# Stick-breaking heads scored in pairs, their recurrence sums taken from two rounded parts

## The chip, the cores and the metric

One core of a Trainium2 chip runs the whole program. The metric is the device time of one execution in microseconds (us); the median of the runs shown is what the change is judged by.

## What is computed

Two layers on 256 tokens of width 1024. Each is a mixer, a layer norm, a mixture of 16 experts (two chosen for each token) and another layer norm. The change lies in the mixer of layer 0, whose left half is a stick-breaking attention with 8 heads of width 64 over two blocks of 128 queries:

```python
z = jnp.einsum('bqhd,bkhd->bhqk', q[:, q0:kend], k[:, :kend]).astype(jnp.float32) * scale
mask = s[None, :] < t[:, None]
log_1mb = jnp.where(mask, -jax.nn.softplus(z), 0.0)
after = lax.cumsum(log_1mb, axis=3, reverse=True) - log_1mb
w = jnp.where(mask, jnp.exp(jax.nn.log_sigmoid(z) + after), 0.0)
outs.append(jnp.einsum('bhqk,bkhd->bqhd', w.astype(v.dtype), v[:, :kend]))
```

Its right half is a state-space recurrence (S5): 32 groups of 16 channels with 64 complex states, `x_l = a x_(l-1) + B u_l`, `y_l = Re(C x_l) + D u_l`, then gelu and a gate. Both halves meet in one output projection.

## The kernel before

Everything is transposed: channels on the partitions, the 256 tokens in the free dimension. Weights come in tiles of 1 MB (`u`, 20 of them) on SyncE's one DMA queue, in the order of use. Plain f32 matmuls run beside matmuls on fp32r operands: where a product must keep f32's precision at fp32r's cost, the operands are split into a rounded part and a rest (`split`, L195) and multiplied in three steps (`mm3`, L203 to L205).

Layer 0's mixer (`mixer0`) runs in this order on TensorE. First the projections to `u`, `v`, then `k` and `q` in four pieces of 128 rows, two heads in each (L986). Then the attention and the recurrence, woven into each other, up to L958, where the recurrence's output is made. Then the output projection (L203 to L205), the gate and the rest of the projection.

The attention comes from `stick`, which returns three functions.
- `scores(h)`, called `S(h)`: one head's logits in a bank of PSUM (`z`, from the pool `acc` of 4 banks). Two matmuls on 64 rows, the upper half of the partitions or the lower, and two bf16 matmuls that add the mask (L1223). ScalarE takes Abs, Exp and Ln of it (L1226, L1228, L1229), VectorE makes the softplus `sp` (L1230), a tile of 128x384 f32 in the pool `b2` of 12 tiles.
- `weights(h)`, `W(h)`: three f32 matmuls with the constant matrices `ntri` sum `sp` over the keys on top of `z` (L1235), ScalarE takes Exp (L1240).
- `values(hp)`, `O(hp)`: four matmuls for two heads, one head to each half of a bank's partitions (L1251), from the pool `mm` of 4 banks.

The recurrence goes by `s5_transpose` (32 transposes on TensorE, L896, in eight banks of `mm` that ScalarE empties, L897), `s5_inputs` (64 matmuls of 32 columns into two banks, L906), `s5_states` and `s5_output` (L958). `s5_states` is a generator on VectorE with six steps, each drawn by one `n(states)`: the first two turn the inputs (L921 to L923), the next two are scans (L930, L932), the fifth and the sixth write the real and the imaginary half of the states `X` (L921 to L923 again, on 128x496). `X` lies in the upper half of the tile `vx`, which held the rows of `u` and then the block matrix of the kernel before.

A scheduler sets each engine's order from the order in which the calls are written, the dependences and the pools; every engine then works through its own list in order, and a wait at its head holds what stands behind. `follow` adds an order between two instructions: `self.cut` holds a split's second part (L195) behind the instruction that it names.

## Time and profile before

| | us |
|---|---|
| median of 3 runs (763.88 to 766.96) | 764.04 |
| the profiled execution | 768.54 |
| its span, first instruction to last | 766.9 |
| TensorE busy in the span | 743.6 |
| VectorE, ScalarE, GpSimd busy | 327.9, 207.2, 46.6 |

How to read it: the page gives each engine's busy time, the span in 40 slices, and the groups of instructions with the mean duration of one. A matmul's duration includes its way through the array, so matmuls overlap, and what one costs in a row of them is the distance from its start to the next one's. An f32 matmul stands in the trace as two records. The timeline merges neighbours of one kind into a row: start, length, number, and in brackets the idle time before it. PE is TensorE, DVE is VectorE, ACT is ScalarE, POOL is GpSimd, SP is SyncE.

### The profile page before, as it was taken

What the parts mean: (1) busy time and instruction counts of PE and PEld (TensorE: products, weight loads), DVE (VectorE), ACT (ScalarE), POOL (GpSimd) and SP (SyncE); (2) the same over time, 40 slices, a digit from 0 to 9 for tenths busy, and PEclk for the clock granted to TensorE, in tenths of its full rate; (3) what the DMA queues carried; (4) which work ended last, traced back from release to release, by engine and by line L of the source; (5) the groups of instructions that cost most, each with busy time, mean ns of one, the idle gap of its engine ahead of it and who ended that gap; (6) DMA issues with size and microseconds to landing.
All of it is one profiled execution on the core that took longest, in us unless ns stands there. A gap on an engine that the chain in (4) does not pass through costs nothing. (4 is left out here: it accounts for less than half of the span.)

```text
span 766.9 us, 10505 instructions
## 1 busy us (share of the span) xinstructions
PE 743.6 (97%) x4115; PEld 419.7 (55%) x4115; DVE 327.9 (43%) x836; ACT 207.2 (27%) x421; POOL 46.6 (6%) x45
## 2 busy tenths in 40 slices
PE   8999999999999999999999999999999999999993
PEld 6588778643534335343878665677535335344332
DVE  9992647711222112124947798835312112221123
ACT  1344435212102001002625575733111001011002
POOL 1010000001000000000020142200002000000000
PEclk9999999999999999999999998999999999999998
DMA  8839879889999999999985100298799999999941
GB/s 322 303 111 195 310 272 409 308 279 378 396 424 421 420 421 421 421 417 421 420 309 194 56 1 0 70 399 306 245 361 417 383 421 421 423 420 420 421 171 59
DMA packets 42539, 241.00 MB, mean 314 GB/s; under 512 B 8144, under 2 KB 9680, under 8 KB 15568
## 3 DMA queue, kind: packets, MB, share of 16 engines
q1 hardware_dynamic: 42480, 240.23, 80.1%
q8 instruction: 34, 0.56, 0.3%
q14 instruction: 25, 0.20, 0.1%
HBM read 238.38 MB, written 1.84 MB: 313 GB/s over the span
## 5 line engine op out<-in xcount | busy, mean ns | idle before, releaser
L493 PE MATMUL mm<-u,s 128*64 128x512 f32 x960 | 214.3, 595 | 0.0
L493 PEld LDWEIGHTS mm<-u,s 128*64 128x64 f32 x960 | 66.6, 137 | 129.6 <-issue 121.7
L523 PE MATMUL mm<-u,b 128*64 128x512 f32 x512 | 113.1, 593 | 0.0
L528 ACT ACTIVATE b<-mm,gslot 128x512 fp32r<-128x512 f32 x32 | 22.0, 687 | 259.3 <-PE mm L523 259.3
L529 DVE SCALAR_TENSOR_TENSOR b<-mm,gslot,b 128x512 fp32r<-128x512 f32 x32 | 24.0, 751 | 146.5 <-ACT b L528 146.5
L523 PEld LDWEIGHTS mm<-u,b 128*64 128x64 f32 x512 | 36.3, 137 | 72.0 <-issue 70.2
L195 DVE TENSOR_TENSOR s<-u,s 128x1024 fp32r<-128x1024 f32 x37 | 45.9, 1248 | 29.4 <-ACT s L192 29.3
L572 DVE TENSOR_TENSOR b<-b,mm 128x256 f32<-128x256 f32 x32 | 12.0, 417 | 91.7 <-PE mm L493 72.7
L192 ACT ACTIVATE s<-u 128x1024 fp32r<-128x1024 f32 x37 | 38.7, 1056 | 43.6 <-PE acc L205 30.6
L986 PE MATMUL mm<-u,u 128*128 128x256 f32 x208 | 46.5, 381 | 1.9 <-DMA u<-w_in 1.9
L986 PEld LDWEIGHTS mm<-u,u 128*128 128x128 f32 x208 | 39.0, 190 | 9.0 <-issue 1.9
L354 ACT ACTIVATE s<-mm,c_k_all 128x256 f32<-128x256 f32 x32 | 18.1, 564 | 81.6 <-PE mm L469 81.6
L203 PE MATMUL acc<-s,u 128*128 128x512 f32 x96 | 38.7, 403 | 0.5 <-ACT u L1206 0.5
L469 PE MATMUL mm<-b,u 128*128 128x256 f32 x160 | 39.1, 326 | 0.0
L205 PE MATMUL acc<-s,u 128*128 128x512 f32 x96 | 38.3, 399 | 0.0
L204 PE MATMUL acc<-s,u 128*128 128x512 f32 x96 | 38.3, 398 | 0.0
L534 PE MATMUL acc<-b,b 128*128 128x512 f32 x128 | 33.5, 399 | 0.0
L469 PEld LDWEIGHTS mm<-b,u 128*128 128x128 f32 x160 | 29.9, 190 | 6.6 <-issue 4.9
L592 DVE COPY b<-mm 128x512 f32<-128x512 f32 x16 | 11.1, 692 | 46.3 <-PE mm L591 46.2
L534 PEld LDWEIGHTS acc<-b,b 128*128 128x128 f32 x128 | 22.6, 189 | 7.8 <-issue 3.2
L356 DVE TENSOR_SCALAR s<-mm,c_k_all 128x256 f32<-128x256 f32 x32 | 16.8, 542 | 22.9 <-PE mm L469 22.7
L469 PE MATMUL mm<-b,s 128*128 128x256 f32 x96 | 23.5, 285 | 0.0
(309 smaller groups left out, 1010.5 us busy)
## 6 DMA issues: line engine op xcount, KB each, us to landing
u<-moe SPq DMA_DIRECT2D x180, 1024.0 KB, 12.5
u<-w_in SPq DMA_DIRECT2D x26, 1024.0 KB, 16.1
u<-w_in SPq DMA_DIRECT2D x10, 512.0 KB, 6.7
s<-moe SPq DMA_DIRECT2D x4, 1024.0 KB, 5.7
b<-moe SPq DMA_DIRECT2D x16, 256.0 KB, 8.2
u<-moe SPq DMA_DIRECT2D x8, 512.0 KB, 16.8
u<-xT SPq DMA_DIRECT2D x4, 256.0 KB, 5.5
out<-u SPq DMA_DIRECT2D x4, 256.0 KB, 4.4
```

The source lines that it names most:

```text
L192: a = self.nc.scalar.activation(s[:, 0], x, AF.Copy)
L195: self.mark = self.nc.vector.tensor_tensor(s[:, 1], x, s[:, 0].bitcast(F32), ALU.subtract)
L203: mm(o, l[0], r[0], start=first, stop=False, skip_group_check=True)
L204: mm(o, l[0], r[1], start=False, stop=False, skip_group_check=True)
L205: self.tail = mm(o, l[1], r[0], start=False, stop=last, skip_group_check=True)
L469: nc.tensor.matmul(pg[:, 0:T], x[:, t, k * P:(k + 1) * P], g.bitcast(F32) if m == 1 else g, start=(i == 0), stop=(i == 2 * m - 1))
L493: self.mark = nc.tensor.matmul(h[c * 64:(c + 1) * 64], xe[:, k, e + c], w[c], start=(k == 0), stop=(k == KC - 1))
L523: self.mark = nc.tensor.matmul(y[c * 64:(c + 1) * 64], hx[:, f, c * 64:(c + 1) * 64], w[:, c * 512:c * 512 + 512], start=(f == 0), stop=(f ...
L528: nc.scalar.activation(yh, y, AF.Copy, scale=gs)
L529: nc.vector.scalar_tensor_tensor(yl, y, gs, yh.bitcast(F32), ALU.mult, ALU.subtract)
L534: self.tail = nc.tensor.matmul(out[half][t], sT[:, t * P:(t + 1) * P], yy, start=False, stop=(p == 7 and j == 1), skip_group_check=True)
L986: self.mark = self.nc.tensor.matmul(ps, w[:, k * P:k * P + P], xT[:, k], start=(k == 0), stop=(k == KC - 1))
```

## The change

`scores` takes a pair of heads, `hp`. Both heads' first parts (256 columns) are issued one behind the other, one on the upper 64 rows and one on the lower, then both second parts (128 columns), then the four mask matmuls. VectorE rounds each head's `sp` to fp32r (`hi`) and takes the rest (`lo`), two tiles of `b2` more for each head; the pool has 15 tiles for 12. `weights` multiplies each of the three column ranges by `hi` and by `lo`, six fp32r matmuls for three f32 ones, against `tr`, an fp32r copy of `ntri` that ScalarE makes once. The weights' Exp is written over `sp`. The calls stand in another order: the first half of the pairs before the third piece of `k` and `q`, all scores before the recurrence's inputs, and `self.cut` is set to the last `lo` of the first two pairs. Five `n(states)` stand where there were six, so that the sixth step, which writes the imaginary half of `X`, is not issued; the readers of that half find what the tile held.

```diff
@@ -33,7 +33,7 @@
 NOSYNC = mybir.DependencyInfo(mybir.DependencyClass.NoSync, mybir.DependencyReason.DATA)
 NU = 20
 NS = 3
-N2 = 12
+N2 = 15
 WARM = 3
 ORD = {mybir.EngineType.PE}
 WARM0 = 5
@@ -1150,21 +1150,21 @@
         self.s5_toeplitz(self.s5_kernel(ca, vx[:, 1].rearrange("p (a r n) -> p a r n", a=16, r=2)), kts)
         S(0), S(1)
         kq(2)
-        S(2), S(3)
-        kq(3)
-        W(0), S(4)
+        cols(k_out(3))
+        W(0), W(1)
+        cols(q_out(3))
+        S(2), W(2), W(3)
         self.s5_transpose(bbp[0], w1t[0])
-        W(1), S(5)
+        S(3)
         self.s5_transpose(bbp[1], w1t[1])
-        O(0), W(2)
+        O(0)
         self.stage(10)
         ps = self.s5_inputs(U, w1t)
         self.issue(CAP[1])
         states = self.s5_states(ps, X, bbp[1].rearrange("p a d h -> p (a d h)").rearrange("p (j n) -> p j n", j=4))
         ys = self.s5_output(U, X, kts, ca, w1t[0].rearrange("p a n -> p (a n)"))
         n = lambda g: next(g, None)
-        n(states), W(3), O(1), S(6), n(states), W(4), n(states), S(7), n(states), W(5), O(2), n(states), W(6), n(states)
-        W(7), O(3)
+        n(states), W(4), W(5), O(1), n(states), W(6), W(7), n(states), O(2), n(states), O(3), n(states)
         self.table("sigmoid_and_others")
         n(ys), n(ys)
         yT = n(ys)
@@ -1212,31 +1212,46 @@
 
         nc = self.nc
         st = {}
-
-        def scores(h):
-            s = slice((h % 2) * 64, (h % 2) * 64 + 64)
-            z = self.acc()
-            k, q = kT[s, h // 2], qT[s, h // 2]
-            nc.tensor.matmul(z[:, 0:T], k[:, 0:P], q, start=True, stop=False, skip_group_check=True)
-            nc.tensor.matmul(z[:, T:T + P], k[:, P:T], q[:, P:T], start=False, stop=False, skip_group_check=True)
-            for c in (0, T):
-                nc.tensor.matmul(z[:, c:c + P], self.identb, self.negb, start=False, stop=False, skip_group_check=True)
-
-            sp = self.b2((P, 384))
-            a = nc.scalar.activation(sp, z[:, 0:384], AF.Abs)
-            self.follow(a, self.logs)
-            nc.scalar.activation(sp, sp, AF.Exp, scale=-1.0)
-            nc.scalar.activation(sp, sp, AF.Ln, bias=1.0)
-            nc.vector.scalar_tensor_tensor(sp, z[:, 0:384], 0.0, sp, ALU.max, ALU.add)
-            st[h] = (z, sp)
+        tr = self.b2((P, 2, P), F32R)
+        nc.scalar.activation(tr, self.ntri, AF.Copy)
+
+        def scores(hp):
+
+            zs = [self.acc() for _ in range(2)]
+            rows = [slice(c * 64, c * 64 + 64) for c in range(2)]
+            for part in range(2):
+                for z, s in zip(zs, rows):
+                    k, q = kT[s, hp], qT[s, hp]
+                    if part == 0:
+                        nc.tensor.matmul(z[:, 0:T], k[:, 0:P], q, start=True, stop=False, skip_group_check=True)
+                    else:
+                        nc.tensor.matmul(z[:, T:T + P], k[:, P:T], q[:, P:T], start=False, stop=False, skip_group_check=True)
+            for z in zs:
+                for c in (0, T):
+                    nc.tensor.matmul(z[:, c:c + P], self.identb, self.negb, start=False, stop=False, skip_group_check=True)
+            for c, z in enumerate(zs):
+
+                sp = self.b2((P, 384))
+                hi, lo = [self.b2((P, 384), F32R) for _ in range(2)]
+                a = nc.scalar.activation(sp, z[:, 0:384], AF.Abs)
+                self.follow(a, self.logs)
+                nc.scalar.activation(sp, sp, AF.Exp, scale=-1.0)
+                nc.scalar.activation(sp, sp, AF.Ln, bias=1.0)
+                nc.vector.scalar_tensor_tensor(sp, z[:, 0:384], 0.0, sp, ALU.max, ALU.add)
+                nc.vector.tensor_copy(hi, sp)
+                low = nc.vector.tensor_tensor(lo, sp, hi.bitcast(F32), ALU.subtract)
+                if hp < 2:
+                    self.cut = low
+                hl = (hi, lo, sp)
+                st[hp * 2 + c] = (z, hl)
 
         def weights(h):
-            z, sp = st[h]
-            mm = lambda o, l, r, stop: nc.tensor.matmul(z[:, o[0]:o[1]], l, r, start=False, stop=stop, skip_group_check=True)
-            mm((0, T), self.ntri[:, 0], sp[:, 0:T], False)
-            mm((P, T), self.ntri[:, 1], sp[:, T:T + P], True)
-            mm((T, T + P), self.ntri[:, 0], sp[:, T:T + P], True)
-            w = self.b2((P, 384))
+            z, hl = st[h]
+            for o, l, c, n in ((0, 0, 0, T), (P, 1, T, P), (T, 0, T, P)):
+                for j in range(2):
+                    nc.tensor.matmul(z[:, o:o + n], tr[:, l], hl[j][:, c:c + n], start=False, stop=o > 0 and j == 1,
+                                     skip_group_check=True)
+            w = hl[2]
             nc.scalar.activation(w, z[:, 0:384], AF.Exp)
             st[h] = w
```

What the scheduler makes of it, at three places. TensorE, behind the recurrence kernel's matmuls (L869): before, head by head (`acc_478` and `acc_488` are the logits of heads 0 and 1, `u_255` holds `k` and `q`, `c_k_bits` the mask):

```order
L1220 MATMUL acc_478<-u_255 128x256
L1221 MATMUL acc_478<-u_255 128x128
L1223 LDWEIGHTS c_k_bits
L1223 MATMUL acc_478<-c_k_bits 128x128
L1223 LDWEIGHTS c_k_bits
L1223 MATMUL acc_478<-c_k_bits 128x128
L1220 MATMUL acc_488<-u_255 128x256
L1221 MATMUL acc_488<-u_255 128x128
```

TensorE at the same place after it (`acc_480` and `acc_481` are heads 0 and 1):

```order
L1226 MATMUL acc_480<-u_255 128x256
L1226 MATMUL acc_481<-u_255 128x256
L1228 MATMUL acc_480<-u_255 128x128
L1228 MATMUL acc_481<-u_255 128x128
L1231 LDWEIGHTS c_k_bits
L1231 MATMUL acc_480<-c_k_bits 128x128
L1231 LDWEIGHTS c_k_bits
L1231 MATMUL acc_480<-c_k_bits 128x128
```

The two heads' matmuls on 64 rows now stand side by side, and the mask matmuls on all rows follow for both. The second pair stands right behind.

TensorE behind the recurrence's inputs (L906), before: the sums of head 3 (L1235), and between the four value matmuls of heads 2 and 3 (L1251, `mm_744`) the scores of head 6 (`acc_751`):

```order
L1235 MATMUL acc_531<-b_54_536,b_14_237 128x256
L1235 MATMUL acc_531<-b_54_536,b_14_237 128x128 x2
L1251 MATMUL mm_744<-b_73_652,u_249 64x256
L1220 MATMUL acc_751<-u_255 128x256
L1251 MATMUL mm_744<-b_83_742,u_249 64x256
L1251 MATMUL mm_744<-b_73_652,u_249 64x128
L1251 MATMUL mm_744<-b_83_742,u_249 64x128
L1221 MATMUL acc_751<-u_255 128x128
```

TensorE at the values of heads 2 and 3 after it (`mm_820`; `hi` is `b_73_616`, `lo` is `b_74_617` of head 5, `b_82_673` and `b_83_674` are those of head 6, `b_36_375` is `tr`):

```order
L1252 MATMUL acc_597<-b_73_616,b_36_375 128x128
L1252 MATMUL acc_597<-b_74_617,b_36_375 128x128
L1266 MATMUL mm_820<-b_55_518,u_249 64x256
L1266 MATMUL mm_820<-b_58_527,u_249 64x256
L1266 MATMUL mm_820<-b_55_518,u_249 64x128
L1266 MATMUL mm_820<-b_58_527,u_249 64x128
L1252 MATMUL acc_662<-b_82_673,b_36_375 128x256
L1252 MATMUL acc_662<-b_83_674,b_36_375 128x256
```

No score stands behind L906 any more, and the value matmuls of all four pairs stand together. Before, those of three pairs were parted, once by a score and twice by a matmul of L259.

VectorE at the recurrence's end, before: the scans, two heads' softplus (L1230), and the fifth and the sixth step (`u_249` holds `X`), then the rests of the values (L1253):

```order
L930 SCALAR_TENSOR_TENSOR u_251<-b_12_234,u_251 128x512
L1230 SCALAR_TENSOR_TENSOR b_86_756<-acc_751,b_86_756 128x384
L932 SCALAR_TENSOR_TENSOR u_251<-b_12_234,u_251 128x512
L1230 SCALAR_TENSOR_TENSOR b_89_776<-acc_771,b_89_776 128x384
L921 TENSOR_TENSOR u_251<-u_251,u_84 128x16x31
L922 TENSOR_TENSOR u_251<-u_251,u_84 128x16x31
L923 TENSOR_TENSOR u_249<-u_251 128x16x31
L921 TENSOR_TENSOR u_251<-u_251,u_84 128x16x31
L922 TENSOR_TENSOR u_251<-u_251,u_84 128x16x31
L923 TENSOR_TENSOR u_249<-u_251 128x16x31
L1253 TENSOR_TENSOR u_256<-mm_642,u_256 128x256
```

VectorE from the scans on after it:

```order
L930 SCALAR_TENSOR_TENSOR u_251<-b_12_234,u_251 128x512
L932 SCALAR_TENSOR_TENSOR u_251<-b_12_234,u_251 128x512
L921 TENSOR_TENSOR u_251<-u_251,u_84 128x16x31
L922 TENSOR_TENSOR u_251<-u_251,u_84 128x16x31
L923 TENSOR_TENSOR u_249<-u_251 128x16x31
L1268 TENSOR_TENSOR u_256<-mm_714,u_256 128x256
```

The two softplus are gone from here (all eight stand ahead of the scans, one rounding and one rest of head 7 between the first steps of the recurrence), and of the two times three products of the last two steps three are left. Behind L958 the lists of TensorE, VectorE, ScalarE and GpSimd read alike before and after, to the end of the program. On SyncE's queue one half-tile of the projection's weights moves from ahead of the 16 small transfers of the recurrence kernel to behind them.

## Rows read from the trace of the kernel before

**Rows 1.** The page: TensorE's busy share in 40 slices.
```profile
PE   8999999999999999999999999999999999999993
```
**Rows 2.** TensorE's waits from 50 to 151 us: total, times, longest.
```profile
PE mm L345 <- DVE u L304: 0.8, 1, 0.8
...
PE acc L1220 <- ACT b L1240: 0.2, 1, 0.2
```
**Rows 3.** Busy time by stretch: engines, granted clock, DMA share, GB/s.
```profile
83.50:99.20 15.70, 15.70 (x103) 11.73 (x99) 12.53 (x20) 7.57 (x16) 0.00 (x0) 1.00 0.80 276
...
220.00:340.00 120.00, 120.00 (x592) 50.21 (x590) 21.89 (x49) 13.12 (x22) 0.00 (x0) 1.00 1.01 421
```
**Rows 4.** Timeline of TensorE: sums of head 0, scores of head 4.
```profile
69.94 1.04 PE L1235 MATMUL acc<-b,b 128*128 128x256 f32 x6
70.81 0.71 PE L896 MATMUL mm<-c_k_all,u 128*128 128x128 f32 x5
71.56 0.70 PE L1220 MATMUL acc<-u 64*128 64x256 f32 x2
...
72.40 0.28 PE L1223 MATMUL acc<-c_k_bits 128*128 128x128 bf16 x2
72.53 1.37 PE L896 MATMUL mm<-c_k_all,u 128*128 128x128 f32 x11
```
**Rows 5.** Timeline of TensorE: values whole, values parted by a score, the recurrence's output.
```profile
77.77 0.87 PE L1251 MATMUL mm<-b,u 128*64 128x256 f32 x8
78.57 1.14 PE L1235 MATMUL acc<-b,b 128*128 128x256 f32 x6
79.64 3.92 PE L906 MATMUL mm<-u,u 128*64 128x32 f32 x128
...
84.57 0.65 PE L1251 MATMUL mm<-b,u 128*64 128x256 f32 x2
85.15 0.70 PE L1220 MATMUL acc<-u 64*128 64x256 f32 x2
85.77 0.86 PE L1251 MATMUL mm<-b,u 128*64 128x256 f32 x6
86.57 0.48 PE L1221 MATMUL acc<-u 64*128 64x128 f32 x2
...
99.21 7.48 PE L958 MATMUL mm<-u,u 128*32 128x128 f32 x192
```
**Rows 6.** Timeline of TensorE: fp32r matmuls in the experts (each one record).
```profile
193.01 0.46 PE L505 MATMUL mm<-R,b 128*128 128x160 f32 x2
193.29 0.32 PE L469 MATMUL mm<-b,s 128*128 128x256 f32 x1
193.45 0.28 PE L469 MATMUL mm<-b,u 128*128 128x256 f32 x1
193.57 0.28 PE L469 MATMUL mm<-b,s 128*128 128x256 f32 x1
```
**Rows 7.** Timeline of ScalarE: what one costs among others.
```profile
73.59 0.52 ACT L1228 ACTIVATE b<-b 128x384 f32<-128x384 f32 x1
74.00 0.60 ACT L897 ACTIVATE u<-mm 128x512 f32<-128x512 f32 x1
74.48 0.53 ACT L1229 ACTIVATE b<-b 128x384 f32<-128x384 f32 x1
```
**Rows 8.** Timeline of VectorE: the recurrence's begin and its sixth step.
```profile
83.50 0.69 DVE L921 TENSOR_TENSOR u<-mm,u 128x512 f32<-128x512 f32 x1 [3.52 <-PE mm L906]
...
93.70 0.67 DVE L921 TENSOR_TENSOR u<-u,u 128x496 f32<-128x496 f32 x1
...
94.99 0.67 DVE L923 TENSOR_TENSOR u<-u 128x496 f32<-128x496 f32 x1
```
**Rows 9.** VectorE's groups from 50 to 99 us: busy, mean ns, idle before.
```profile
L1230 DVE SCALAR_TENSOR_TENSOR b<-acc,b 128x384 f32<-128x384 f32 x8 | 4.4, 554 | 17.5 <-ACT b L1229 17.5
```
**Rows 10.** Timeline of SyncE's queue: the experts' first loads; the next layer's first.
```profile
75.61 49.65 SPq L144 DMA_DIRECT2D u<-moe  x17
...
337.19 7.87 SPq L144 DMA_DIRECT2D u<-w_in  x5
```

## The prediction

> **What bounds the kernel now.** The page's slices come first: TensorE stands at 9 in all but the first and the last [rows 1]. Then its waits in the stretch that the change touches: from 50 us to the first expert the list is a few tenths, 0.2 us of it in the attention [rows 2]. Between 83.50 and 99.20 us TensorE is busy for all 15.70 us, at the full granted clock of 2.4 GHz (1.00) [rows 3]. So here the end is set by TensorE's own list, and what an edit is worth is the distance from start to start that it takes out of that list, less the waits that it brings in. The other engines have room: VectorE is busy 12.53 and ScalarE 7.57 of the 15.70 us.
>
> Behind L958 the lists of four engines read alike before and after, so the time up to L958's start (99.21 us [rows 5]) decides. What follows hangs on it: TensorE's order, buffers that it frees, loads that wait for those. The other limit is the loads. In the experts they run at 421 GB/s, and TensorE is busy for 120 of 120 us all the same [rows 3]. I come to that among the rivals.
>
> **Scores in pairs.** Head 4 takes 71.56 to 72.53, 0.97 us: 0.84 to the first mask matmul at 72.40, then 0.13 for two of those [rows 4]. What the columns themselves cost is told by head 0's sums, 512 columns in 0.87 us [rows 4], so 1.70 ns a column, and 0.65 us for the 384 columns of a score. So about 0.2 of the 0.84 goes for changing between matmuls on 64 and on 128 rows. In a pair both heads share this: 0.84 and four mask matmuls, 0.24, make 1.08 us, if the two heads' matmuls run at once. No row shows two matmuls on different rows at once. The bounds: one after the other, a pair takes 1.08 + 0.65 = 1.73 us, against 1.94 now, and the four pairs save 0.8 us. Fully at once they save 4 x 0.86 = 3.4 us. I take 3.4, by the nearest row: the values of heads 0 and 1 go to different halves of a bank's partitions, issued in turns as the scores now are, and 768 columns in all, which at 1.70 ns would take 1.30 us, take 0.80 with the change of mode (77.77 to 78.57 [rows 5]). That is full overlap.
>
> The Trainium skill, "TensorE: Matmul & The Clock Gate", Part 3 (packing small matmuls), says that matmuls on different groups of rows run at the same time, and gives 3.07 times for four of them. By it the pairs save the 3.4 us as well; no run so far shows it for rows.
>
> **Sums from two parts.** Before: three f32 matmuls, 0.87 us a head [rows 4]. After: two fp32r matmuls of 256 columns and four of 128. At 256 columns one costs 0.12 us (193.45 to 193.57 [rows 6]). At 128 no row shows the price; the nearest is two of 160 columns, 193.01 to 193.29, 0.14 each with the change of mode from what stands ahead [rows 6]. The bounds are 0.06, half of 0.12, and 0.14. I take 0.11, near the row with few columns: 0.24 + 0.44 = 0.68 us a head, 0.19 saved, 1.5 us for eight. By the bounds it is 0.5 to 3.1 us.
>
> The Trainium skill speaks against more than that: in the same page, section "LDWEIGHTS", the time to load weights goes by the columns of the weights (128 columns, 107 ns) and not by those that stream through. By it each 128-column matmul costs 0.107 us, and the saving is 1.5 us; by the stream alone it would be 3.1. The two matmuls of 160 columns agree with it.
>
> **Order on TensorE.** Now a score of head 6 stands between the values of heads 2 and 3: they take 84.57 to 85.15 and 85.77 to 86.57, 1.38 for 0.80 us, and the score's first part 0.62 for some 0.53 [rows 5]. That is 0.67 us for one parted group. Three of four groups are parted in the listing (one by a score, two by a matmul of the projection's residual), after it none: 2.0 us, and 0.1 for the last two groups, which now stand side by side. Sums that stand alone between values or L906 cost 1.07 (78.57 to 79.64 [rows 5]) instead of 0.87, by the change of columns. Four heads do so now; after it two groups of two remain: 0.5 us saved. The waits on ScalarE at scores go: 0.2 [rows 2], and 0.2 at 70.81 to 71.56, where five transposes take 0.75 us, though eleven last 1.37 and five 0.71 to their ends, so one costs 0.11 [rows 4]. In all 3.0 us.
>
> **What is added.** First, a wait on ScalarE. Its list behind the third pair's scores has 18 instructions up to the seventh copy of a transposed bank (L897): Abs, Exp, Ln of heads 4, 5 and half of 6, two weights' Exp, seven copies. L906's second bank is the one that this copy frees. Two cost 0.89 us (73.59 to 74.48 [rows 7]), so 18 cost 8.0. TensorE brings 7.4 us of work to that point: two heads' sums 1.4, 32 transposes 3.5, the fourth pair 1.1, values 0.9, nine matmuls of L906 0.5. It waits 0.6 us, and some 0.4 more for the hand-overs between the engines; I take 1.0, between 0.5 and 1.5. Behind it wait all of L906 and the recurrence.
>
> Second, VectorE. Sixteen instructions of 128x384, roundings and rests. The row of that shape is L1230's 0.55 us [rows 9]; the bounds are half of this and a little over it, 4 to 9 us in all. Twelve of them run while VectorE idles (17.5 us of idle time ahead of L1230 alone [rows 9]) and cost nothing. If that cover were gone, the splits (L195) would be late, which are first read at L958's side. Two of head 7 fall between L906's end and the states. From L906 (83.50) to the states' last write (94.99 + 0.67) there are 12.2 us now [rows 8]. The sixth step, 93.70 to 95.66, goes, 2.0; two softplus of 0.55 and their waits go, 1.1 to 1.5; a rounding and a rest come, 0.6 to 1.1. That leaves 9.3 to 10.2 us. TensorE needs 15.7 us now from L906's end to L958 [rows 5]. Of these go the two scores (1.9), the parted groups (2.1), 4.35 + 0.4 of five heads' sums for 2.7 of four: 9.6 us. So the states are ready about when they are wanted, and L958's second stage waits 0 to 0.7 us; I take 0.2. Without the sixth step's removal it would be 2 us. That is what is late next here.
>
> Third, things at nothing: the copy of `ntri` on ScalarE, idle at that time; three more tiles of `b2`; the half-tile that moves behind the 16 small loads on SyncE's queue. It is read behind L958 only; the experts' loads behind it move by one half-tile's 1.25 us (0.5 MB at 421 GB/s).
>
> **The sum.** 3.4 + 1.5 + 3.0 = 7.9 us saved (2.0 for the values and 0.1, 0.5, 0.4 make the 3.0), less 1.0 and 0.2: 6.7 us. The profiled execution took 768.54 us, its span 766.9, so 1.6 lie around it, which the change doesn't touch: it would take 761.8. The runs' median is 764.04, 4.5 below; I take the saving over as it is, since the stretch from 83.50 to 99.20 ran at the full clock. From the median: **757.3 us**.
>
> **The rivals.**
> Forecast, 0.60: 755.8 to 758.8.
> *The pairs don't overlap.* Then the scores save 0.8 instead of 3.4, but the fourth pair hides in the wait on ScalarE: 2.0 us less, 759.3. For it: no row with different row groups. Against it: the values' overlap [rows 5]. 0.14.
> *More than that.* Narrow fp32r matmuls at 0.06 us save 1.6 more, the waits on ScalarE and the states may come out at 0.5: 754.5. 0.11.
> *The loads take it back.* At 421 GB/s the first layer's 96 tiles of 1.05 MB need 239 us. They are issued from 75.61 us on, and all are issued by 337.19, so the queue has at least 22 us of slack [rows 3, 10]. The first of them come ahead of most of the gain. If the rest kept their old times too, TensorE would reach the last experts ahead of their weights and wait there: 761 to 764. Against it: after 99 us every load waits for a buffer that a matmul or a split frees, and moves with them. 0.11.
> *Slower: fp32r at f32's price.* If a matmul on `hi` or `lo` took an f32 matmul's columns, 1.70 ns each, 1024 columns a head would take 1.74 us for 0.87. The place is L1252, eight heads: 8.5 us more than forecast, 765.8. It decides from 0.25 us a matmul on, against my mean of 0.11 (48 x 0.14 us are the 6.7). The fp32r rows at 0.12 speak against it [rows 6]. With pairs that don't overlap it is 767.8 or more. 0.04.
> *The change doesn't do what it says* would be the scores again head by head; the listing shows them in pairs, and what is left of that is the first rival.
>
> **How the numbers follow.** The likeliest is 757.3. The runs of the kernel differ by 3.1 us (763.88 to 766.96), so half a per cent, 3.8 us, is what a measurement can tell from no change: faster means below 760.2, slower above 767.9. Faster: forecast, no overlap and more than that, with a little off for scatter, 0.82. Same: the loads, and the slower rival where the pairs overlap, 0.15. Slower: that rival with pairs that don't, and scatter, 0.03. The range leaves out the slower rival and most of the loads: 754.3 to 760.9.
>
> **What would show it.** L958 starts at 92 to 93 us instead of 99.21. A pair of scores takes 1.1 us from its first matmul to what follows; 1.7 means no overlap. Six matmuls of sums take 0.7 us a head. TensorE shows a wait of about 1 us for L897 at L906 or at the values, and at most 0.7 for L923 in L958. The distance from L958 to the last instruction stays at 667.7 us of the span (766.9 - 99.2); if it grows by some us with waits for `moe` loads, the loads took the gain. I am wrong if L958 comes early and that distance grows, or if L958 comes no earlier.

## The result and the profile after

| | before | after |
|---|---|---|
| median of 8 runs, us | 764.11 (763.54 to 766.96) | 758.04 (756.22 to 760.46) |
| profiled execution, us (its span) | 768.54 (766.9) | 759.68 (757.8) |
| first score of the attention | 51.85 | 51.82 |
| L906 starts, ends | 79.64, 83.5 | 77.97, 82.3 |
| L958 starts | 99.21 | 91.55 |
| what follows L958 starts | 106.62 | 99.42 |
| first expert's matmul (L493) | 151.32 | 144.02 |

The ratio is 0.9907, with a 95% interval of 0.9886 to 0.9928. The change saves 6.1 us by the medians. The executions of either kernel fall on two levels some 3 us apart (six of 8 at 763.5 to 764.3 and two at 766.9 before; four at 756.2 to 756.8 and four at 759.3 to 760.5 after), so a median mixes them; level against level the saving is 7.3 us. The traces below show what goes with the levels. The places in the program are steadier than the times, and I go by them.

The page of the changed kernel, TensorE's busy share and its granted clock in 40 slices, beside [rows 1]:

```profile
PE   7999999999999999999999999999999999999993
...
PEclk9999999999999999999999998999999999999998
```

TensorE's timeline after (start, busy time, line, form, count), which answers to [rows 4, 5]; from the fourth pair's scores to what follows L958:

```profile
73.74 0.70 PE L1226 MATMUL acc<-u 64*128 64x256 f32 x4
74.28 0.39 PE L1228 MATMUL acc<-u 64*128 64x128 f32 x4
74.60 0.40 PE L1231 MATMUL acc<-c_k_bits 128*128 128x128 bf16 x4
74.83 2.04 PE L896 MATMUL mm<-c_k_all,u 128*128 128x128 f32 x16
77.08 0.87 PE L1266 MATMUL mm<-b,u 128*64 128x256 f32 x8 [0.21 <-ACT u L897]
77.97 4.36 PE L906 MATMUL mm<-u,u 128*64 128x32 f32 x128
82.26 1.58 PE L1252 MATMUL acc<-b,b 128*128 128x256 f32 x12
83.77 0.87 PE L1266 MATMUL mm<-b,u 128*64 128x256 f32 x8
84.57 1.58 PE L1252 MATMUL acc<-b,b 128*128 128x256 f32 x12
86.08 1.52 PE L1266 MATMUL mm<-b,u 128*64 128x256 f32 x16
87.53 3.84 PE L259 MATMUL acc<-c_k_all,u 128*128 128x128 f32 x32
91.13 0.47 PE L203 MATMUL acc<-s,u 128*128 128x512 f32 x1
91.55 7.95 PE L958 MATMUL mm<-u,u 128*32 128x128 f32 x192
99.42 0.50 PE L204 MATMUL acc<-s,u 128*128 128x512 f32 x1
```

A pair of scores with its masks takes 74.83 - 73.74 = 1.09 us; one head took 0.97 before [rows 4]. Two heads' sums take 83.77 - 82.26 = 1.51 us, or 1.40 where no values stand ahead. The values stand whole: 0.80 us, and 1.45 for the last two groups side by side. Two things got longer. L906 takes 4.29 us from start to start (3.86 before), and the sixteen transposes ahead of the values 2.25 (1.86 for the sixteen at 71.88): 0.8 us in all. I read this as waits for ScalarE's copies of the banks (L897); the timeline marks 0.21 us of it so, and the kernel with heads apart, below, bears it out. And L958 takes 7.87 us from start to start instead of 7.41.

VectorE at the end of the recurrence, after, beside [rows 8]:

```profile
82.25 0.69 DVE L921 TENSOR_TENSOR u<-mm,u 128x512 f32<-128x512 f32 x1 [0.87 <-PE mm L906]
...
90.48 0.68 DVE L923 TENSOR_TENSOR u<-u 128x496 f32<-128x496 f32 x1
91.08 1.08 DVE L1268 TENSOR_TENSOR u<-mm,u 128x256 fp32r<-128x256 f32 x3
```

The last write of the states ends at 91.16, 8.9 us behind L906's end and 0.4 us ahead of L958. Then come the rests of the values (L1268). By the trace the first of them, which ends at 91.49, releases L958's first loading of weights: its bank of `mm` is the one that held the values of the first pair. But this holds L958 for next to nothing: it starts 0.42 us behind L203, and in the kernel before, where nothing held it, 0.41. What L958 lost stands behind its first four loadings of weights. These loadings before:

```profile
99.20 0.16 PEld L958 LDWEIGHTS mm<-u,u 128*32 128x32 f32 x8 [0.24 <-issue]
```

and after:

```profile
91.55 0.14 PEld L958 LDWEIGHTS mm<-u,u 128*32 128x32 f32 x4 [0.25 <-DVE u L1268]
91.99 0.17 PEld L958 LDWEIGHTS mm<-u,u 128*32 128x32 f32 x4 [0.30 <-DMA u<-moe]
```

The eight that ran in a row are now parted by 0.30 us. The trace puts this down to a load of `moe`, which L958 doesn't read; I put it down to L958's list of waits, eight instructions that only wait for a semaphore. Before, all eight stood ahead of L958, at 97.0 to 97.8; now four of them stand inside it, at 91.55 to 91.92. Behind L958 the stretches are as before: to the first expert 44.6 us after and 44.7 before, and between 220 and 340 us TensorE is busy for all 120, with the loads at 420 GB/s, as in [rows 3].

The spans of the two profiled executions differ by 9.1 us, 1.8 more than the first expert's start. The granted clock explains 1.7 of that: 10.2 us at half clock before and 6.8 after. Stretches by engine (PE, PEld, DVE, ACT, POOL), then granted clock, DMA share and GB/s; two of the kernel before:

```profile
381.80:385.20 3.40, 3.40 (x10) 2.66 (x10) 1.86 (x4) 1.53 (x2) 0.00 (x0) 0.50 1.02 423
467.10:474.00 6.90, 6.90 (x30) 3.73 (x31) 5.27 (x16) 2.95 (x14) 1.04 (x1) 0.51 0.00 0
```

and the only such stretch of the kernel after between 5 and 750 us:

```profile
458.20:465.00 6.80, 6.80 (x28) 3.63 (x29) 5.06 (x14) 2.74 (x13) 1.04 (x1) 0.50 0.00 0
```

### The profile page after: what moved, and what is told of

Same layout as the page of the kernel before. It is cut to its first block, busy times and chain, and to the rows that moved or that the text cites. A ratio compares the mean times of both kernels' runs of the same rounds, so it can differ in the third digit from the quotient of the medians.

```text
span 757.8 us, 10531 instructions
## 1 busy us (share of the span) xinstructions
PE 733.8 (97%) x4115; PEld 413.9 (55%) x4115; DVE 333.1 (44%) x849; ACT 207.5 (27%) x422; POOL 46.8 (6%) x45
## 5 line engine op out<-in xcount | busy, mean ns | idle before, releaser
L493 PE MATMUL mm<-u,s 128*64 128x512 f32 x960 | 214.3, 595 | 0.0
L493 PEld LDWEIGHTS mm<-u,s 128*64 128x64 f32 x960 | 66.7, 137 | 129.6 <-issue 122.3
L192 ACT ACTIVATE s<-u 128x1024 fp32r<-128x1024 f32 x37 | 38.7, 1056 | 42.0 <-PE acc L205 28.9
L203 PE MATMUL acc<-s,u 128*128 128x512 f32 x96 | 38.0, 396 | 0.5 <-ACT u L1206 0.5
L205 PE MATMUL acc<-s,u 128*128 128x512 f32 x96 | 37.8, 394 | 0.0
L204 PE MATMUL acc<-s,u 128*128 128x512 f32 x96 | 37.5, 391 | 0.0
```

Source lines behind the costliest of these rows:

```text
L192: a = self.nc.scalar.activation(s[:, 0], x, AF.Copy)
L203: mm(o, l[0], r[0], start=first, stop=False, skip_group_check=True)
L204: mm(o, l[0], r[1], start=False, stop=False, skip_group_check=True)
L205: self.tail = mm(o, l[1], r[0], start=False, stop=last, skip_group_check=True)
L493: self.mark = nc.tensor.matmul(h[c * 64:(c + 1) * 64], xe[:, k, e + c], w[c], start=(k == 0), stop=(k == KC - 1))
```

## Experiments

Every kernel below is the changed one with the edit shown. As there, the imaginary half of the states is not written, except where the sixth step is back. The table has the places by the traces and the medians (lowest to highest) of the timed runs. The kernel before was timed again beside each of the three sets of experiments: 764.35, 767.23 and 765.08 us by the medians, 763.4 to 763.7 at the lowest. So medians of different sets differ by more than some of the effects, and the ratios given below are to the kernel before in the same set.

| kernel | L958's end | first expert | us |
|---|---|---|---|
| before | 106.62 | 151.32 | 764.11 (763.54 to 766.96) |
| after | 99.42 | 144.02 | 758.04 (756.22 to 760.46) |
| heads apart | 102.05 | 146.63 | 759.41 (758.59 to 763.09) |
| sums in f32 | 100.64 | 145.24 | 760.51 (757.55 to 760.95) |
| order alone | 103.49 | 148.12 | 761.15 (760.19 to 765.31) |
| sixth step back | 106.18 | 151.97 | 765.54 (758.98 to 770.02) |
| four matmuls | 102.49 | 147.99 | 760.01 (756.13 to 760.68) |
| bank early | 99.04 | 146.43 | 761.95 (760.57 to 763.18) |
| copies on VectorE | 98.84 | 143.42 | 757.33 (755.14 to 760.94) |
| complete, orders by hand | 96.69 | 140.79 | 756.73 (752.83 to 757.67) |
| the same less the sixth step | 96.00 | 140.07 | 752.98 (752.52 to 753.40) |
| sixth step, covered | 97.62 | 142.67 | 757.69 (755.09 to 759.54) |

### The parts undone, one by one

Heads apart:

```diff
-            for part in range(2):
-                for z, s in zip(zs, rows):
...
-            for z in zs:
+            for z, s in zip(zs, rows):
+                k, q = kT[s, hp], qT[s, hp]
+                nc.tensor.matmul(z[:, 0:T], k[:, 0:P], q, start=True, stop=False, skip_group_check=True)
+                nc.tensor.matmul(z[:, T:T + P], k[:, P:T], q[:, P:T], start=False, stop=False, skip_group_check=True)
                 for c in (0, T):
```

> The changed kernel with one part undone: the two heads of a pair are scored one behind the other, each with its own two mask matmuls behind it (as in the kernel before, it leaves nothing more out than the changed kernel, which doesn't write the imaginary half of the states). Theory (the pair's matmuls run at once): a pair takes 1.9 us instead of 1.08; the fourth pair stands ahead of the 0.9 us wait for ScalarE's copies and is hidden there, so the first L204 matmul starts 2.5 to 3.4 us later than in the changed kernel (99.42), at 101.9 to 102.8. Rival (the pairing only moves the waits): the pair's time grows, but the waits on ScalarE shrink by as much, and L204 starts within 0.5 us of 99.42.

TensorE's timeline of the fourth pair, heads apart:

```profile
76.68 0.70 PE L1224 MATMUL acc<-u 64*128 64x256 f32 x2
77.21 0.38 PE L1225 MATMUL acc<-u 64*128 64x128 f32 x2
...
78.71 1.92 PE L896 MATMUL mm<-c_k_all,u 128*128 128x128 f32 x16
```

A pair takes 78.71 - 76.68 = 2.03 us, against 1.09. The first row says why: one head's first part (two records) takes 0.53 us to the next row, and in the changed kernel both heads' (four records) take 0.54. The two heads' records start 7 ns apart there. So the overlap is whole. Four pairs are 3.8 us; 2.6 of them arrive at L958's end and at the first expert. The rest is given back: the waits for L897 go (the transposes take 1.85 us again and L906 3.87), 0.8 us, and L958 is 0.2 us shorter. The theory held.

Sums in f32:

```diff
-                nc.vector.scalar_tensor_tensor(sp, z[:, 0:384], 0.0, sp, ALU.max, ALU.add)
-                nc.vector.tensor_copy(hi, sp)
-                low = nc.vector.tensor_tensor(lo, sp, hi.bitcast(F32), ALU.subtract)
+                low = nc.vector.scalar_tensor_tensor(sp, z[:, 0:384], 0.0, sp, ALU.max, ALU.add)
...
-                for j in range(2):
-                    nc.tensor.matmul(z[:, o:o + n], tr[:, l], hl[j][:, c:c + n], start=False, stop=o > 0 and j == 1,
-                                     skip_group_check=True)
+                nc.tensor.matmul(z[:, o:o + n], self.ntri[:, l], hl[0][:, c:c + n], start=False, stop=o > 0,
+                                 skip_group_check=True)
```

> The changed kernel with the other part undone: sums by three f32 matmuls of sp, no hi and lo on VectorE (the imaginary half of the states is left out as in the changed kernel). Theory: a head's sums take 0.87 us instead of 0.70, 1.2 to 1.5 us over eight heads, of which the second pair-and-third pair's share ahead of the ScalarE wait is hidden; L204 starts at 100.2 to 100.8 instead of 99.42, although VectorE's list in the recurrence gets shorter by a rounding and a rest (0.36 + 0.56). Rival (VectorE's list is what ends last): L204 starts at 98.9 to 99.4, as the 0.9 us off VectorE's list count more.

Two heads' sums, f32:

```profile
71.02 1.97 PE L1246 MATMUL acc<-b,b 128*128 128x256 f32 x12
72.83 1.91 PE L896 MATMUL mm<-c_k_all,u 128*128 128x128 f32 x16
```

1.81 us for two heads against 1.40: 0.2 a head, 1.6 us for eight, of which 1.2 arrive at L958's end and at the first expert. The changed kernel has sixteen instructions more on VectorE, and they don't turn this round. The theory held.

Both undone, with the two edits above:

> Both undone: heads scored one by one, sums in f32, and only the order of the calls of the changed kernel (with its five steps of the states; the imaginary half is left out as there). Theory (parts add up; the order is worth some 3 us): L204 starts 3.4 to 4.4 us later than 99.42, at 102.8 to 103.8, and still 2.8 to 3.8 ahead of the kernel before (106.62). Rival (the order is worth nothing without the pairs): 105.8 to 106.6.

L958 ends 3.1 us ahead of the kernel before and 4.1 behind the changed one, where the two parts alone make 2.6 + 1.2 = 3.8. They add up within 0.3, and the order of the calls, with the sixth step left out as in the changed kernel, is worth 3.1.

### The sixth step

```diff
-        n(states), W(4), W(5), O(1), n(states), W(6), W(7), n(states), O(2), n(states), O(3), n(states)
+        n(states), W(4), W(5), O(1), n(states), W(6), W(7), n(states), O(2), n(states), O(3), n(states), n(states)
```

> The changed kernel with the sixth step of the states put back, so that both halves of the states are written and nothing is left out. Theory (VectorE's list ends last at L958): three instructions of 0.67 us stand ahead of the values' rests, L958 starts at 93.5 instead of 91.55 and L204 at 101.2 to 101.5. Rival (the step is hidden behind L259 and the first stage of L958): L204 within 0.5 us of 99.42.

TensorE's timeline at L958, with the wait ahead of it:

```profile
93.91 10.31 PE L958 MATMUL mm<-u,u 128*32 128x128 f32 x160 [1.95 <-DVE u L1268]
```

The stretches around it (last three numbers: granted clock, DMA share, GB/s):

```profile
94.00:95.60 1.60, 1.58 (x32) 0.76 (x32) 0.85 (x3) 0.00 (x0) 0.00 (x0) 1.00 0.71 220
95.60:100.00 4.40, 4.40 (x72) 2.35 (x72) 0.00 (x0) 0.06 (x1) 0.00 (x0) 0.50 0.92 385
100.00:109.30 9.30, 9.30 (x103) 5.43 (x97) 4.74 (x8) 2.21 (x4) 0.00 (x0) 0.50 0.30 107
```

L958 starts 2.4 us later, where 2.0 were expected. What neither theory had is what follows. TensorE stands for 1.95 us, and 1.7 us after it starts again the granted clock falls to 0.50 (1.2 GHz) and stays there for 13.7 us. L958 takes 12.3 us instead of 7.9, and the first expert starts 8.0 us later, behind that of the kernel before. The median is 765.54; the ratio to before is 0.9992 (0.9959 to 1.0026). In eight of ten executions the mean clock was 0.986 or lower; the changed kernel's eight had 0.989 to 0.997. One had 0.990 and took 763.13. One had 0.997, and that one took 758.98, 2.2 to 2.8 above the lower level of the changed kernel, about the wait alone. So **the gain of the changed kernel hangs on the step that it leaves out**: with both halves of the states written, and nothing else changed, nothing of it is left in the median; only the one execution with a mean clock of 0.997 kept most of it.

### What stands in front of L958

Four matmuls for a head's sums:

```diff
-            for o, l, c, n in ((0, 0, 0, T), (P, 1, T, P), (T, 0, T, P)):
+            for o, l, c, n in ((0, 0, 0, T + P), (P, 1, T, P)):
```

> The changed kernel with four matmuls a head for the sums instead of six: the two column ranges that use the same weights (columns 0 to 255 and 256 to 383) go in one matmul of 384 columns each for hi and lo (nothing more is left out than in the changed kernel, the imaginary half of the states). In the changed kernel a 128-column fp32r matmul takes 0.06 us behind one of 256 columns and 0.11 behind one of 128. Theory (the weights' load of 0.107 us is what a narrow matmul waits for, and TensorE's list in front of L958 is no longer what ends last): a head's sums take 0.52 us instead of 0.68 to 0.70, 1.3 us less over eight heads, but behind L906 this only makes a longer wait at L958 for VectorE's values' rest (0.5 to 1.0 us), and L204 starts at 98.8 to 99.5 instead of 99.42. Rival (TensorE's list still decides): L204 at 98.0 to 98.3. Rival on the price (time goes by columns): a head takes 0.66 us or more.

TensorE's timeline, two heads' sums, the last sums and values, and the middle of L958:

```profile
70.36 1.35 PE L1252 MATMUL acc<-b,b 128*128 128x384 f32 x8
71.54 1.93 PE L896 MATMUL mm<-c_k_all,u 128*128 128x128 f32 x16
...
83.61 1.04 PE L1252 MATMUL acc<-b,b 128*128 128x384 f32 x5
84.49 0.38 PE L259 MATMUL acc<-c_k_all,u 128*128 128x128 f32 x2
...
87.37 3.62 PE L259 MATMUL acc<-c_k_all,u 128*128 128x128 f32 x30
90.74 0.48 PE L203 MATMUL acc<-s,u 128*128 128x512 f32 x1
...
97.94 4.62 PE L958 MATMUL mm<-u,u 128*32 128x128 f32 x67 [1.32 <-issue]
```

and a stretch behind it:

```profile
98.20:105.00 6.80, 6.80 (x73) 4.18 (x71) 2.79 (x5) 0.99 (x2) 0.00 (x0) 0.50 0.37 117
```

Two heads take 1.18 us instead of 1.40, 0.11 a head less: most of what the price by weights' loads says, and not the 0.66 of the other. Of 0.9 us for eight heads L958 starts only 0.4 earlier, at 91.16, but not for a longer wait for VectorE, as the theory had it: L958 stands 0.42 us behind L203, as in the changed kernel and in the one before. Up to the second pair's values TensorE is 0.96 us ahead (82.81 for 83.77). Then the order costs it: sums and two matmuls of L259 part the values of the last pairs, and from 83.61 to the rest of L259 it takes 3.76 us where the changed kernel takes 2.96. So TensorE's own list still decided here. L958's end tells nothing: within it TensorE stands for 1.32 us, for nothing that the profile shows ("issue"), and 0.3 us after it goes on the clock falls for 6.8 us. What it waited for stays open. In time the kernel is no better than the changed one (lowest 756.13 against 756.22). The theory did not hold, and its rival's time could not be read.

The bank freed early:

```diff
+            if hp == 0:
+                t = self.b2((P, T))
+                nc.vector.tensor_copy(t, o[:, 0:T])
+                o = t
```

> The changed kernel, but VectorE copies the first pair's values out of their bank (128x256, 0.4 us) in the recurrence, so that the bank that L958 writes first no longer waits for the rest that stands behind the recurrence (the imaginary half of the states is left out as in the changed kernel). Theory (the bank, and not the states, holds L958 back by 0.4 us): L958's first matmuls start ahead of L259, and its many waits with them; L204 starts at 98.9 to 99.2 instead of 99.42, since the states come 0.4 us later. Rival (the states hold it): 99.4 to 99.9.

TensorE's timeline:

```profile
87.53 0.41 PE L958 MATMUL mm<-u,u 128*32 128x128 f32 x4
87.88 3.84 PE L259 MATMUL acc<-c_k_all,u 128*128 128x128 f32 x32
91.64 7.47 PE L958 MATMUL mm<-u,u 128*32 128x128 f32 x188
99.04 0.50 PE L203 MATMUL acc<-s,u 128*128 128x512 f32 x1
```

and its longest wait behind L958:

```profile
PE mm L203 <- ACT u L1186: 1.7, 1, 1.7
```

The first four records of L958, with their list of waits, go ahead of L259, and L958 ends at 99.04 instead of 99.42. But that is not a gain of 0.4 us: the L203 that stood ahead of L958 now stands behind it, and it costs 0.23 in a row. The first L204 starts at 99.38, for 99.42, which is in neither expected range, and the next L203, where both kernels have done the same work, at 99.84 for 99.99. So freeing the bank is worth 0.15 us. The states didn't hold L958 either: they were written at 91.49, and no wait for them is in its list. And the first expert starts 2.4 us later. In ScalarE's list one weight split more (L192, at 111.39) now stands ahead of the splits of y (L1186), and TensorE waits 1.7 and 0.7 us for these. The scheduler that orders the lists took that turn for a copy of 0.4 us at 84.19.

Copies on VectorE (`dve` names two of the four banks of each half):

```diff
-            nc.scalar.activation(o[:, q * 4:q * 4 + 4].rearrange("p a n -> p (a n)"), pt, AF.Copy)
+            d = o[:, q * 4:q * 4 + 4].rearrange("p a n -> p (a n)")
+            if q in dve:
+                nc.vector.tensor_copy(d, pt)
+            else:
+                nc.scalar.activation(d, pt, AF.Copy)
```

> The changed kernel with four of the eight copies of transposed banks on VectorE instead of ScalarE (the imaginary half of the states is left out as in the changed kernel). Theory (TensorE waits some 0.9 us for ScalarE's copies around L906, and the recurrence behind it sets L958): L906 ends 0.7 to 0.9 us earlier, at 81.2 to 81.4, and L204 starts at 98.5 to 98.8 instead of 99.42. Rival (the wait only moves to the softplus that VectorE now does later): L204 at 99.2 to 100.

TensorE's timeline at the first pair's values:

```profile
77.48 0.87 PE L1270 MATMUL mm<-b,u 128*64 128x256 f32 x8 [0.67 <-DVE u L899]
```

What follows L906 (here L910) starts at 81.99 instead of 82.26, and L958 ends at 98.84, 0.6 us earlier: 0.3 of it came in front of L958, and 0.3 within it (7.58 us for 7.87). L906 is short again, 3.81 us, but most of the wait moved to the values ahead of it, where TensorE now waits 0.67 us for VectorE's copy. Neither expectation holds alone.

### A complete kernel

A first kernel with the whole computation took the last three edits, the sixth step, and L958 by stages (the loop over `st` outside that over `m`):

> The complete computation, nothing left out: the changed kernel with the sixth step of the states put back, and four parts against the wait that it brings: copies of transposed banks half on VectorE, sums by four matmuls a head, the first values' bank freed early, and L958 done stage by stage (all matmuls of the first stage, which need no states, then those on the real half, then those on the imaginary half). Theory (the sixth step costs much because TensorE stands for 1.95 us at L958 and its clock then goes to 0.5 for 13.7 us; when other work covers the step it costs nothing): no wait of more than 0.4 us ahead of or in L958, the granted clock stays at 1.0 from 50 to 300 us, L958 takes some 1 us less for fewer changes between 128 and 64 rows, and L204 starts at 95.5 to 97.5; 752 to 755 us at the clock of the faster runs. Rival (VectorE's list still ends last): a wait of over 1 us in L958, the clock falls behind it, L204 at 101 or later and 760 us or more.

Its L958 opened a bank with each of the sixteen matmuls of the first stage where it must be opened once, so its sums in L958 are not those of the reference; the instructions are the same in number and kind. There was no wait at L958, the clock stayed at 1.00 through it, and it ended at 96.58. Then the gain went again: TensorE waits 0.8 us at the transposes of y (L978), and further on (timeline)

```profile
111.33 0.50 PE L203 MATMUL mm<-u,s 128*128 128x256 f32 x2 [1.68 <-ACT u L1190]
```

with this stretch behind it:

```profile
113.20:116.60 3.40, 3.40 (x17) 3.40 (x18) 0.84 (x2) 0.00 (x0) 0.00 (x0) 0.50 1.01 422
```

These are the same splits as in the bank-early kernel, here with half the clock behind them. The first expert started at 146.22, and the median was 758.90 us (758.55 to 761.12) for the 752 to 755 expected. The next three opened the bank once. Two of them also set two orders by hand, the place of the transposes of y (`n(ys)`) and that of the weight split that had come ahead of the splits of y; the third has only the second of these:

```diff
-        yT = n(ys)
...
-        self.jobs(self.jobs_out(lhs, ((0, 0), (0, 1)), out))
+        js = self.jobs_out(lhs, ((0, 0), (0, 1)), out)
+        self.jobs(js[:2])
+        yT = n(ys)
+        self.jobs(js[2:])
...
-            nc.scalar.activation(h[0], hb[:, k], AF.Copy)
+            self.behind = nc.scalar.activation(h[0], hb[:, k], AF.Copy)
```

> The complete computation, nothing left out: the kernel of the run before (sixth step back, half of the banks' copies on VectorE, sums by four matmuls a head, the first values' bank freed early, L958 stage by stage, where now only the first matmul into a bank opens it), with two orders set by hand behind L958: the transposes of y stand behind the second job of the projection, and the third weight split on ScalarE behind the splits of y. Theory (those two orders gave back 2.4 us and 0.8 us of the last run's gain, and the half clock at 113 us followed from the waits): no wait of TensorE over 0.6 us between 50 and 125 us, granted clock 1.0 from 50 to 300 us, the first expert starts at 141.0 to 142.0 instead of 144.02 in the changed kernel; 753.3 to 754.5 us in the faster runs. Rival (the chain of gelu, transposes and splits on VectorE and ScalarE now ends last): the first expert at 143 to 144.5, no faster than the changed kernel.

> The same kernel without the sixth step, so that the imaginary half of the states is left out again, and nothing else. Theory (a covered step costs nothing): the first expert starts within 0.5 us of the complete one. Rival (the step costs its own 2 us on VectorE): 1.5 to 2 us earlier.

> The complete computation, nothing left out: the changed kernel with the sixth step back, and only the cover for it: the first values' bank freed early, L958 stage by stage, and the third weight split behind the splits of y; copies on ScalarE and sums by six matmuls as in the changed kernel. Theory (the step is dear only where TensorE stands for it): a wait of at most 0.6 us in L958, no half clock between 90 and 120 us, the first expert at 142.6 to 144.0 instead of the 152.0 that the step cost uncovered. Rival (the step costs 2 us wherever it stands, and the clock falls): 147 or later.

The complete one, its stretches up to 120 us:

```profile
50.00:90.00 40.00, 39.96 (x430) 34.78 (x430) 30.91 (x48) 25.04 (x50) 2.33 (x2) 1.00 0.75 217
90.00:97.00 7.00, 7.00 (x198) 5.97 (x197) 5.78 (x12) 1.11 (x2) 0.00 (x0) 1.00 0.94 367
97.00:120.00 23.00, 22.48 (x125) 19.14 (x124) 18.05 (x27) 13.70 (x23) 0.00 (x0) 1.00 1.01 420
```

its longest wait of TensorE up to 120 us:

```profile
PE acc L203 <- ACT u L1212: 0.5, 1, 0.5
```

and L958 (here L962) in its timeline, without its first four matmuls:

```profile
90.88 5.89 PE L962 MATMUL mm<-u,u 128*32 128x128 f32 x188
```

Between 50 and 120 us only the 0.5 at L203 is left, which the changed kernel has too, and the first expert starts at 140.79: 3.2 us ahead of the changed kernel and 10.5 ahead of the one before, with the whole computation. Its ratio to before is 0.9876 (0.9844 to 0.9909). Less the sixth step it starts at 140.07, 0.72 earlier, but there the first pair's scores already started 0.66 us earlier (51.36 for 52.02, ahead of anything that the edit touches), so the covered step costs some 0.06. The medians are 3.7 us apart all the same. Five of the six executions of the complete kernel had a mean clock of 0.990 to 0.992, and none of the four less the step, which had 0.995 or more; the complete kernel's one execution at 0.996 took 752.83, as short as those. Whether the step has a part in that stays open. The third kernel has only the cover: its first expert is at 142.67, where the bare step has 151.97, although TensorE waits 0.8 us for y at the transposes, and none of its four executions had a mean clock under 0.990. 1.6 us of that distance is L958 by stages (below); the rest says that the bare step is dear because TensorE stands for it. The theories held at the places: the complete kernel's first expert came 0.2 us ahead of its range, and the 0.5 us of the second held once the earlier start is taken off. In time only one of the six executions of the complete kernel came down to the 753.3 to 754.5 expected, at 752.83. L958 by stages is shorter by itself: 188 records take 5.8 us to what follows in all three, and 7.4 in the bank-early kernel. Between matmuls on 128 and on 64 rows it changes once in a bank instead of seven times: 1.6 us for twelve changes, 0.13 each.

## Why the prediction was right, and where it was not

**What bounds.** TensorE's own list in front of L958 was the limit: what came out of it came out at L958's start (7.66 us), at its end (7.20, since L958 got 0.46 longer) and at the first expert (7.3).

**Scores in pairs.** I had 1.08 us a pair, and it takes 1.06 to 1.09. The rival without overlap falls. The term was 3.4 us; with heads apart in the new order a pair takes 2.03 us instead of the 1.94 that I took, so it is 3.8. The Trainium skill's sentence ("TensorE: Matmul & The Clock Gate", Part 3) that matmuls on different groups of rows run at once agrees: here two take 0.54 us where one takes 0.53.

**Sums.** I expected 0.68 us a head and 1.5 us in all; it measured 0.70 to 0.75, and 1.6 us against f32 in the same order, of which 1.2 arrive at L958's end. The price of a narrow fp32r matmul, for which I took 0.11 between 0.06 and 0.14, is both: in the trace's single records one costs 0.06 behind a matmul of 256 columns and 0.11 behind one of 128. The Trainium skill (same page, section "LDWEIGHTS") has the load of weights go by their columns; for 128 columns its formula gives an estimate of 107 ns. The 0.11 behind a narrow matmul agrees with that. That the load hides behind a wide matmul is my reading of the 0.06, and the kernel with four matmuls a head, which takes 0.59, fits it.

**Order.** I expected 3.0 us; it is worth 3.1 alone.

**The wait on ScalarE.** I expected 1.0 us and measured 0.8, at the place named. That it is a wait for ScalarE, and that it grows as scores get shorter, is shown by the kernel with heads apart, where it is gone.

These four close at L958's start: 3.8 + 1.6 + 3.1 less 0.8 make 7.7 us against 7.66. I had 3.4 + 1.5 + 3.0 less 1.0, 6.9, so L958 came earlier than the 92 to 93 us that I named.

**VectorE's end.** I had 0.2 us with bounds 0 to 0.7, as a wait for the states in L958's second stage. L958 got 0.46 longer, but that the size fits is luck, for no such wait is there: the states took 8.9 us from L906's end, less than my 9.3 to 10.2, and were written 0.4 us before L958 began. What got longer is L958's first part, where its list of waits, which before stood ahead of it, now parts its first loadings of weights. With the bank of the first values freed early, L958's first records and their list of waits go ahead of L259, and that is worth 0.15 us.

**The sum.** I forecast 6.7 us; it is 7.3 at the first expert and level against level, and 6.1 by the medians. The forecast was 757.3 us and the median 758.04. That these are so near is in part chance: no execution took between 756.8 and 759.3, and the median lies in that gap. One slip in the working: the rival with more gain comes to 755.0 by its own terms (757.3 less 1.6 and 0.7), not 754.5.

**The step that failed** is the sentence "Without the sixth step's removal it would be 2 us". At L958's start it was 2.4, but 8.0 at the first expert and 7.5 in the median, with 13.7 us at half clock behind the wait. I priced the wait and not what the clock does behind it. The rival on that was missing: with the step, the change ends where it began. **The loads** took nothing back, as argued: L958's end to the first expert is 44.6 us in the changed kernel and 44.7 in the one before.

**The distance from L958 to the end** was to stay at 667.7 us; it is 666.2. The profiled execution before had 10.2 us at half clock within it and the one after 6.8, which is 1.7 us of work, and L958 got 0.46 longer.

## What to carry over

Where TensorE is the bound, look for what stands late on the next engine before you count a gain: a wait of 2 us behind a shortened list cost 8 here, because the granted clock fell behind it. Cover a late producer by placing work that doesn't need it in front, as the first stage of L958 is here, instead of shortening the list further. After each edit compare the lists of all engines far behind it: a copy of 0.4 us moved a split that stands 27 us behind it, and 2.4 us went with that. And before a place that comes earlier is called a gain, see that the same work lies ahead of it: the bank freed early seemed to win 0.4 us, and 0.23 of that was one matmul that had changed sides.

## What the runs showed of the hardware

**Half the clock after short waits, not always, and once without one.** Falls of the granted clock to 0.50 came 1.7 us after TensorE went on from a wait of 1.95 us (sixth step), 0.3 us after one of 1.32 (four matmuls), and 0.7 us after the second of two of 1.68 and 0.72 (the first kernel with the whole computation). The kernel with the bank early had two waits of the same size at the same place and kept the full clock there. The kernel before fell at 381.8 us for 3.4 us though TensorE had been busy for all of the 6.8 us ahead:

```profile
375.00:381.80 6.80, 6.80 (x62) 6.80 (x61) 6.58 (x21) 3.40 (x3) 0.00 (x0) 1.00 1.01 422
```

So a wait makes a fall likelier, as the sixth step's executions show, but it neither brings one each time nor is it needed just ahead.

**The two levels of time** go with such falls. In all 13 profiled executions TensorE waits 1.0 us for VectorE at one place in the second layer. In the complete kernel (timeline):

```profile
452.85 0.38 PE L1514 MATMUL acc<-u,u 128*128 128x256 f32 x1 [1.00 <-DVE u L1407]
```

The clock falls there at 455.1 us for 6.8 us; in the same kernel less the sixth step, with the same wait at 452.16, it doesn't fall between 7 and 743 us. It falls 0.9 to 2.7 us behind this wait in nine of the 13, for 6.8 us in eight of them and for 10.2 in one. 6.8 us at half clock is 3.4 us of work, about the distance between the levels; the changed kernel's fall at 458.2 is this one. What decides whether the fall comes is not known, and whether a kernel without that wait would keep to the lower level was not tried.
